# A value split ordered behind the newest weight split in the scans of a hybrid decoder step

## The chip, the cores and the metric

The kernel runs on one core of a Trainium2 chip. The metric is device microseconds from the start to the end of one execution. A profiled execution of the same program gives the traces.

## The reference

The program computes one inference step of a decoder trunk of one layer: a prompt of 256 tokens and a sample group of 8 sequences of 4 tokens, 288 tokens in all, model width 2048. The layer is a SwiGLU feed-forward block, a mixer, and a second SwiGLU block, each with a norm before and behind it. The mixer projects its input once and runs two groups of recurrences, GLA (4 heads, 128 x 256 state) and HGRN2 (8 heads, 128 x 128 state):

```python
S_t = diag(a_t) S_{t-1} + k_t^T v_t ;  o_t = q_t S_t
```

Each token reads its own update. The outputs are normalised per head, gated, concatenated and projected. Everything is float32. The outputs are both token groups and the final states of both groups; the sample group starts from given states.

## The kernel before, in words

All 288 tokens lie side by side in the free dimension. Matmuls take weights as the stationary 128 x 128 operand and tokens as the moving 128 x 288 operand. To keep float32 accuracy each operand is split into a high part and a low part, and three matmuls (lines 548, 549, 550) make one product.

**Weights.** They come in units of 128 x 1024. A unit is loaded by a DMA that SyncE issues (lines 62 and 64, tile `raw`, 3 buffers), then split: ScalarE copies `raw` to the high part `wh` (L96), and VectorE subtracts for the low part `wl` (L97). The split parts have 4 buffers, so a split waits until TensorE has done with the unit four places before. A unit feeds 24 matmuls.

**Blocks.** `block` multiplies a column block of a weight matrix: it takes the units one after the other, calls a `tick` after each 128 rows, and splits units ahead (`W.ahead`). Its four results stand in four of five PSUM banks until VectorE and ScalarE take them away. In the mixer the blocks are q and k of GLA, v of GLA, then `hfq` (forget gate and query of HGRN2) and `hi` (its values), then four gate blocks and the output projection.

**Scans.** While TensorE works on these blocks, six scans run beside it, two for GLA and four for HGRN2, each for two heads. A scan is a Python generator, and every tick advances the first one in the list by one step. It goes through eight levels: at each level VectorE multiplies decays into `Q` (L1055), `k` (L1058) and `F` (L1060), ScalarE lays copies out for the scores (L1065 and L1070 into the tile `R`), and TensorE makes scores (L995 and others). After the levels, `value_parts` splits the sample's values, then for each of two heads come `key_t` (TensorE turns the keys), `out` (outputs), `key_e` (ScalarE takes the turned keys away: `kd` L1210, `ks` L881), `apart` (VectorE masks by sequence: `bd` L1218) and `sample` (TensorE makes the state update `sn`, L1260 or L1263; VectorE adds it to the state, L1266).

**The value split.** The values of the sample tokens stand in `vs`, 32 partitions, in float32. They come there by ScalarE (L906), or, in the blocks v0, v1 and hi0, by VectorE's 32 x 32 transposes and four DMAs of GpSimd (L924); `Vh` and `Vg` are the prompt's values, moved likewise (L926). `value_parts` writes the high part twice and the low part once into one tile of 96 partitions, `Vsg` or `Vsh`: ScalarE's copy L1197, VectorE's subtraction L1198, ScalarE's copy L1199. The readers are the masked values `bd` in the HGRN scans and the matmuls `sn` in the GLA scans.

**Order.** Engines issue in order. Which order that is a list scheduler decides when the program is built: it goes by the place in the source and by a model of when each instruction could run, and can move an instruction ahead of others that come before it in the source. `tc.issue_after(ins)` adds an edge from each instruction traced in its block to `ins` where both are on the same engine; it sets the order on that engine and adds no wait between engines.

Of the kernel before, what the change touches and what calls it, by code (L numbers as in the profile page):

```python
# [9 lines left out]
F32 = mybir.dt.float32  # L10
F32R = mybir.dt.float32r
U8 = mybir.dt.uint8
AF = mybir.ActivationFunctionType
ALU = mybir.AluOpType
# [4 lines left out]
TS = 32  # L19
# [18 lines left out]
class Weights:  # L38
# [46 lines left out]
    def pieces(self, n):  # L85

        i = self.split
        raw = self.raws.pop(i)
        pool = self.extra if i in self.extra_units else self.hlp
        h = pool.tile([P, 1024], F32R, name=f"wh{i}", tag="wh")  # L90
        l = pool.tile([P, 1024], F32R, name=f"wl{i}", tag="wl")
        self.parts[i] = (h, l)
        self.split += 1
        for c in range(0, 1024, 1024 // n):
            c = slice(c, c + 1024 // n)
            i1 = self.nc.scalar.activation(h[:, c], raw[:, c], AF.Copy).ins  # L96
            i2 = self.nc.vector.tensor_tensor(l[:, c], raw[:, c], h[:, c].bitcast(F32), op=ALU.subtract).ins  # L97
            yield i1, i2

    def room(self):  # L100
# [25 lines left out]
def trunk_kernel(ctx, tc, x_prompt, x_sample, state_gla, state_hgrn, norm_gains, f1_in, f1_out, f2_in, f2_out,  # L126
# [3 lines left out]
    V, S, G, PE = nc.vector, nc.scalar, nc.gpsimd, nc.tensor  # L130
# [40 lines left out]
    W = Weights(tc, rawp, hlp)  # L171
# [604 lines left out]
    def mixer(pn, border):  # L776
        with ExitStack() as mx:
# [170 lines left out]
            def scan(d, Vt, V32, Vs, gla, ytile0, s0, sp_out, ss_out):  # L948
# [9 lines left out]
                fs, c = [d["f"]], 0  # L958
# [234 lines left out]
                def value_parts():  # L1193

                    c = slice(0, 512) if gla else slice(0, 256)
                    v = V32[0:TS, c]
                    S.activation(Vs[0:TS, c], v, AF.Copy)  # L1197
                    V.tensor_tensor(Vs[TS:2 * TS, c], v, Vs[0:TS, c].bitcast(F32), op=ALU.subtract)  # L1198
                    S.activation(Vs[2 * TS:96, c], v, AF.Copy)  # L1199

                def key_t(a):
                    tp = auxtile("tp_k")
# [116 lines left out]
                def new_state():  # L1319
                    sample(*todo.pop(0))  # L1320
                    if todo and todo[0][0] in kds:
                        apart(*todo[0])

                value_parts()
                for a in range(2):
                    tp = key_t(a)
# [135 lines left out]
            for kind, g in HORDER:  # L1462
# [8 lines left out]
                for j in list(ds):  # L1471
                    if j // 2 in vts:
                        c = slice((j % 2) * 256, (j % 2 + 1) * 256)
# [116 lines left out]
```

## Time and profile before

| | |
|---|---|
| median of 3 runs | 2254.05 us (2253.89 to 2254.5) |
| profiled execution, span from first to last instruction | 2251.7 us |
| median less span | 2.35 us |
| DMA traffic | 384.28 MB, mean 171 GB/s |
| costliest VectorE group: weight split L97 | 821.8 us in 674 |
| costliest ScalarE group: weight split L96 | 711.4 us in 674 |

The profiled execution has no run time of its own beside its span; the last difference stands for what lies around it. Lines in the fences come from the page of the profile or from views of its trace. A row of a timeline holds the start and the duration in us, the engine (PE is TensorE, PEld its weight loads, DVE is VectorE, ACT is ScalarE, POOL is GpSimd), the source line, the operation with the tile written and the tiles read, and in brackets how long the engine stood idle before it and what ended that. A row of waits holds who waited for whom, the total in us, how often, and the longest.

### The profile page before, as it was taken

How to read it: one execution, taken by the hardware profiler on the slowest of the kernel's cores; microseconds unless marked ns; L12 is line 12 of the kernel's file. 1: busy time of each engine (PE TensorE's matmuls, PEld its weight loads, DVE VectorE, ACT ScalarE, POOL GpSimd, SP SyncE). 2: the span in 40 equal slices, each digit the busy share in tenths (PEclk: the TensorE clock that was granted, in tenths of full speed). 3: DMA queues.
4: the chain of work that ended last, by engine and by line, in shares of the span. 5: the costliest groups of instructions: out<-in, count | busy, mean ns of one | idle time of the engine just before them, and what ended most of it. 6: DMA issues, size and time to landing. Idle time of an engine off the chain costs nothing.

```text
span 2251.7 us, 43317 instructions
## 1 busy us (share of the span) xinstructions
PE 2235.9 (99%) x17832; PEld 2220.0 (99%) x17832; DVE 1384.2 (61%) x2249; ACT 1023.0 (45%) x1551; POOL 170.7 (8%) x311
## 2 busy tenths in 40 slices
PE   9999999999999999999999999999999999999998
PEld 9999999999999999999999999999999999999998
DVE  7545545554565568787888755944555455545646
ACT  6443333333334345665676654543333333333344
POOL 2000000000000001333000000430000000000005
PEclk9999999999999999999999999999999999999999
DMA  7554555555555554667565554655555555555555
GB/s 222 170 163 165 169 166 163 168 166 164 167 168 180 167 169 138 192 205 201 167 176 173 171 187 132 187 185 168 167 163 167 168 163 166 168 167 164 167 166 151
DMA packets 226886, 384.28 MB, mean 171 GB/s; under 512 B 21138, under 2 KB 60736, under 8 KB 226688
## 3 DMA queue, kind: packets, MB, share of 16 engines
q1 hardware_dynamic: 214096, 365.15, 51.0%
q0 software_dynamic: 10416, 16.18, 2.7%
q8 instruction: 140, 2.29, 0.4%
q10 hardware_dynamic: 2176, 0.18, 0.1%
q14 instruction: 58, 0.48, 0.1%
HBM read 363.75 MB, written 11.80 MB: 167 GB/s over the span
## 4 chain that ended last, share of the span: by engine, by line
PE 94%; DVE 2%; ACT 1%; DMA 1%; issue 1%; POOL 0%; DVEq 0%; ACTq 0%; POOLq 0%; SPq 0%
PE gate L548 9%; PE gate L550 9%; PE gate L549 9%; PE up L550 8%; PE up L548 8%; PE out L549 8%; PE up L549 8%; PE out L550 8%; PE out L548 8%; PE mo L550 2%; PE mo L548 2%; PE mo L549 2%; PE hfq L548 1%; PE hfq L549 1%; PE hfq L550 1%; DVE wl L97 1%
## 5 line engine op out<-in xcount | busy, mean ns | idle before, releaser
L97 DVE TENSOR_TENSOR wl<-raw,wh 128x1024 fp32r<-128x1024 f32 (+1 forms) x674 | 821.8, 1220 | 619.2 <-ACT wh L96 615.2
L96 ACT ACTIVATE wh<-raw 128x1024 fp32r<-128x1024 f32 (+1 forms) x674 | 711.4, 1057 | 1021.6 <-PE gate L549 309.9
L548 PE MATMUL gate<-xh,wh 128*128 128x288 f32 x1660 | 489.2, 296 | 0.5 <-DVE z L1484 0.3
L550 PE MATMUL gate<-xh,wl 128*128 128x288 f32 x1660 | 488.7, 295 | 0.5 <-DVE wl L97 0.5
L549 PE MATMUL gate<-xl,wh 128*128 128x288 f32 x1660 | 485.3, 295 | 0.0
L549 PE MATMUL out<-hl,wh 128*128 128x288 f32 x1408 | 415.6, 295 | 0.0
L548 PE MATMUL up<-xh,wh 128*128 128x288 f32 x1408 | 414.9, 295 | 0.3 <-ACT g L618 0.2
L550 PE MATMUL up<-xh,wl 128*128 128x288 f32 x1408 | 415.1, 295 | 0.0
L550 PE MATMUL out<-hh,wl 128*128 128x288 f32 x1408 | 415.0, 295 | 0.0
L549 PE MATMUL up<-xl,wh 128*128 128x288 f32 x1408 | 414.6, 294 | 0.0
L548 PE MATMUL out<-hh,wh 128*128 128x288 f32 x1408 | 413.7, 294 | 0.0
L548 PEld LDWEIGHTS gate<-xh,wh 128*128 128x128 f32 x1660 | 311.0, 188 | 1.7 <-DVE z L1484 0.6
L550 PEld LDWEIGHTS gate<-xh,wl 128*128 128x128 f32 x1660 | 311.4, 188 | 0.9 <-DVE wl L97 0.9
L549 PEld LDWEIGHTS gate<-xl,wh 128*128 128x128 f32 x1660 | 310.4, 188 | 0.3
L548 PEld LDWEIGHTS up<-xh,wh 128*128 128x128 f32 x1408 | 264.1, 188 | 0.9 <-ACT g L618 0.7
L550 PEld LDWEIGHTS out<-hh,wl 128*128 128x128 f32 x1408 | 264.7, 188 | 0.0
L548 PEld LDWEIGHTS out<-hh,wh 128*128 128x128 f32 x1408 | 264.5, 188 | 0.0
L549 PEld LDWEIGHTS out<-hl,wh 128*128 128x128 f32 x1408 | 264.4, 188 | 0.0
L550 PEld LDWEIGHTS up<-xh,wl 128*128 128x128 f32 x1408 | 264.2, 188 | 0.0
L549 PEld LDWEIGHTS up<-xl,wh 128*128 128x128 f32 x1408 | 264.1, 188 | 0.1
L706 DVE TENSOR_TENSOR y<-out,y 128x288 f32<-128x288 f32 x288 | 121.2, 452 | 101.3 <-PE out L550 98.3
L548 PE MATMUL hfq<-xh,wh 128*128 128x288 f32 x256 | 78.1, 305 | 0.0
(391 smaller groups left out, 2516.3 us busy)
## 6 DMA issues: line engine op xcount, KB each, us to landing
raw<-in_ffn_w_in_dram SPq DMA_DIRECT2D x351, 512.0 KB, 3.5
raw<-in_ffn_w_out_dram SPq DMA_DIRECT2D x176, 512.0 KB, 3.5
raw<-in_mix_w_in_dram SPq DMA_DIRECT2D x64, 512.0 KB, 3.9
raw<-in_mix_w_in_dram SPq DMA_DIRECT2D x96, 256.0 KB, 3.1
raw<-in_mix_w_out_dram SPq DMA_DIRECT2D x32, 512.0 KB, 3.7
out_dram<-s POOLq DMA_DIRECT2D x32, 256.0 KB, 2.7
s<-in_state_gla_dram SPq DMA_DIRECT2D x16, 256.0 KB, 5.2
s<-in_state_hgrn_dram SPq DMA_DIRECT2D x16, 256.0 KB, 4.8
```

The lines of the kernel that those rows point to most:

```text
L96: i1 = self.nc.scalar.activation(h[:, c], raw[:, c], AF.Copy).ins
L97: i2 = self.nc.vector.tensor_tensor(l[:, c], raw[:, c], h[:, c].bitcast(F32), op=ALU.subtract).ins
L548: yield lambda: PE.matmul(dst, w[0][:, c:c + P], parts[0], start=start, stop=False)
L549: yield lambda: PE.matmul(dst, w[0][:, c:c + P], parts[1], start=False, stop=False)
L550: yield lambda: PE.matmul(dst, w[1][:, c:c + P], parts[0], start=False, stop=stop)
L706: V.tensor_tensor(y[k], ps, y[k], op=ALU.add)
```

## The change

The weight splitter remembers its newest pair of instructions, and the three instructions of the value split are traced under an edge to that pair:

```diff
             i1 = self.nc.scalar.activation(h[:, c], raw[:, c], AF.Copy).ins
             i2 = self.nc.vector.tensor_tensor(l[:, c], raw[:, c], h[:, c].bitcast(F32), op=ALU.subtract).ins
+            self.recent = i1, i2
             yield i1, i2
...
                     v = V32[0:TS, c]
-                    S.activation(Vs[0:TS, c], v, AF.Copy)
-                    V.tensor_tensor(Vs[TS:2 * TS, c], v, Vs[0:TS, c].bitcast(F32), op=ALU.subtract)
-                    S.activation(Vs[2 * TS:96, c], v, AF.Copy)
+                    with tc.issue_after(W.recent[0]), tc.issue_after(W.recent[1]):
+                        S.activation(Vs[0:TS, c], v, AF.Copy)
+                        V.tensor_tensor(Vs[TS:2 * TS, c], v, Vs[0:TS, c].bitcast(F32), op=ALU.subtract)
+                        S.activation(Vs[2 * TS:96, c], v, AF.Copy)
```

The two copies on ScalarE stand behind the newest `wh`, the subtraction on VectorE behind the newest `wl`. Newest is meant at the place in the source: the last unit that had been split when `value_parts` was traced. No instruction is added or removed. The scheduler, with the new edges, also places some other instructions of the scans differently.

## The prediction

> **What bounds the kernel now.** First the profile page, then the waits of TensorE over the whole span.
>
> ```profile
> span 2251.7 us, 43317 instructions
> PE 2235.9 (99%) x17832; PEld 2220.0 (99%) x17832; DVE 1384.2 (61%) x2249; ACT 1023.0 (45%) x1551; POOL 170.7 (8%) x311
> ...
> PE sc L995 <- ACT R L1070: 2.4, 1, 2.4
> PE warm L297 <- POOL onesD L228: 1.1, 1, 1.1
> PE gate L550 <- DVE wl L97: 0.5, 1, 0.5
> PE gate L548 <- DVE z L1484: 0.3, 1, 0.3
> ```
>
> TensorE is busy for 99% of the span, so an edit on another engine pays only where TensorE stands still or runs slowly. Its waits are a short list. The longest is one wait of 2.4 us, in the scans: the score matmuls of L995 wait for ScalarE's copy R of L1070. The change touches the scans, so I opened the timelines of the four engines around that place, TensorE first (start, duration, engine, line).
>
> ```profile
> 1052.36 0.29 PE L550 MATMUL hfq<-xh,wl 128*128 128x288 f32 x1
> 1055.00 0.55 PE L995 MATMUL sc<-R,k_h 128*32 128x48 f32 x32 [2.35 <-ACT R L1070]
> ...
> 1056.39 0.42 PE L548 MATMUL hfq<-xh,wh 128*128 128x288 f32 x1
> ...
> 1059.90 0.29 PE L548 MATMUL hfq<-xh,wh 128*128 128x288 f32 x1
> ...
> 1060.16 0.29 PE L550 MATMUL hfq<-xh,wl 128*128 128x288 f32 x1
> 1060.38 0.45 PE L995 MATMUL sc<-Q,k_h 128*32 128x16 f32 x32
> ...
> 1061.00 0.30 PE L549 MATMUL hfq<-xl,wh 128*128 128x288 f32 x1
> ...
> 1063.91 0.29 PE L550 MATMUL hfq<-xh,wl 128*128 128x288 f32 x1
> ```
>
> Two losses are seen here. From 1052.36 to 1055.00 nothing starts. And from 1056.39 to 1059.90 the weight matmuls start farther apart. The table by stretches (us, busy and count, granted clock, DMA share, GB/s) says why:
>
> ```profile
> 1056.39:1059.90 3.51, 3.51 (x17) 0.51 0.84 216
> 1061.00:1064.51 3.51, 3.51 (x28) 1.00 0.71 208
> ```
>
> The granted clock fell to half after the gap, and 3.51 us held 17 matmuls where they hold 28 at full clock. Why was R late? ScalarE, VectorE and GpSimd:
>
> ```profile
> 1045.23 1.06 ACT L96 ACTIVATE wh<-raw 128x1024 fp32r<-128x1024 f32 x1 [1.03 <-PE hfq L549]
> 1052.39 0.41 ACT L1197 ACTIVATE Vsh<-vs 32x256 fp32r<-32x256 f32 x1 [6.09 <-DMA vs<-y]
> 1052.71 0.40 ACT L1065 ACTIVATE R<-Q 128x256 f32<-128x256 f32 x1
> ...
> 1053.60 1.04 ACT L96 ACTIVATE wh<-raw 128x1024 fp32r<-128x1024 f32 x1
> 1054.55 0.40 ACT L1070 ACTIVATE R<-Q 128x256 f32<-128x256 f32 x1
> ...
> 1048.47 0.45 DVE L1055 TENSOR_TENSOR Q<-Q,F 128x288 f32<-128x288 f32 x1
> ...
> 1053.14 0.43 DVE L1055 TENSOR_TENSOR Q<-Q,F 128x256 f32<-128x256 f32 x1 [3.42 <-ACT R L1065]
> ...
> 1045.32 2.19 POOL L924 DMA_DIRECT2D vs<-y x4
> ```
>
> ScalarE issues in order. The scheduler had put the value split of the first HGRN scan (L1197) ahead of R (L1065). Its input vs comes by four DMAs that GpSimd issued from 1045.32 on, so ScalarE stood for 6.09 us. Behind it stood L1065, the weight split and L1070, VectorE's Q waited 3.42 us for L1065, and TensorE at last waited for L1070.
>
> **The change, part by part.** No instruction is added or removed. The three instructions of the value split, at six places (two GLA scans, four HGRN scans), get an order edge behind the newest weight split traced before them. In the built order of the changed kernel the value split no longer stands between the weight split at 1045.23 and L1065; in the HGRN scan at issue it now stands after the copy rp (L1127) and ahead of kd (L1210), several scan steps later.
>
> *What goes.* The gap: 1055.00 − 1052.36 = 2.64 us; the ordinary step from a weight matmul to a score is 1060.38 − 1060.16 = 0.22; so 2.42 us go. The slow stretch: 15 starts from 1056.39 to 1059.90, 3.51 us; at full clock 22 starts from 1061.00 to 1063.91 take 2.91, 0.132 each, so 15 take 1.98; 1.53 us go. (The counts of the table agree: 28 − 17 = 11 matmuls, 1.45 us.) Sum **3.95 us**.
>
> [...]
>
> *What is late next at the old place.* L1065 needs Q, done at 1048.47 + 0.45 = 1048.92. In the old rows ScalarE takes 0.89 us from L1065 to the weight split and 0.95 from there to L1070; from 1048.95 on that ends at 1050.79 + 0.40 = 1051.2. That weight split needs a buffer that TensorE gives back, and L1070 stands behind it; its fellow at 1045.23 shows such a wait, and a unit's 24 matmuls at 0.13 us with about 1 us of scores between put the next release, as an estimate, at 1045.2 + 3.2 + 1 = 1049.4, before its turn at 1049.84. TensorE asks at 1052.36 + 0.22 = 1052.58: 1.4 us to spare. The next score (1060.38, in the new time 1056.43) needs k_h, which the new order puts behind another weight split:
>
> ```profile
> 1057.36 1.23 DVE L97 TENSOR_TENSOR wl<-raw,wh 128x1024 fp32r<-128x1024 f32 x1 [0.40 <-ACT wh L96]
> 1058.50 0.42 DVE L1058 TENSOR_TENSOR k_h<-k_h,F 128x256 f32<-128x256 f32 x1
> ```
>
> ScalarE's half of it can start at about 1052.6 and takes 1.06; VectorE's follows at 1053.7; k_h starts 1.14 later and ends at 1055.3, 1.1 us ahead.
>
> *What the moved split costs at its new place.*
>
> ```profile
> L1197 ACT ACTIVATE Vsg<-vs x2: 630/630/631, 924.1 to 984.6; 32x512 fp32r<-32x512 f32 x2
> L1198 DVE TENSOR_TENSOR Vsh<-vs,Vsh x4: 414/416/417, 1054.3 to 1117.5; 32x256 fp32r<-32x256 f32 x4
> L1218 DVE TENSOR_TENSOR bd<-Vsh,bmask x16: 671/681/689, 1059.1 to 1248.0; 96x512 fp32r<-96x512 f32 x16
> ...
> 1070.48 0.39 ACT L1210 ACTIVATE kd<-tp_k 128x256 f32<-128x256 f32 x1 [1.03 <-PE tp_k L877]
> ...
> 1073.07 1.23 DVE L97 TENSOR_TENSOR wl<-raw,wh 128x1024 fp32r<-128x1024 f32 x1 [1.72 <-ACT wh L96]
> ...
> 1182.11 0.45 DVE L1431 SCALAR_TENSOR_TENSOR q_h<-z,lsg 128x288 f32<-128x288 f32 x1
> 1182.60 0.29 DVE L883 TENSOR_TENSOR ks<-tp_k,ks 32x128 fp32r<-32x128 f32 x1
> ...
> 1185.49 0.40 PE L1263 MATMUL sn<-bd,ks 96*128 96x512 f32 x1
> ```
>
> Behind the split on ScalarE wait kd and ks, on VectorE ks and the masked values bd; TensorE's state matmuls sn (L1263) wait for these. In the first HGRN scan ScalarE idles 1.03 us before kd, and two copies of 0.42 fit; VectorE idles 1.72 us, with 0.42 + 2 × 0.68 = 1.78 to place in it and in another gap before: nothing. The third HGRN scan is the tightest that I found: q_h to 1182.5, split to 1183.0, ks to 1183.3, first bd to 1184.0, sn at 1185.49: 1.5 us to spare. In the GLA scans the split takes 0.63 per copy, and sn needs it itself. So nothing at the six places; bounds zero and 2 × 2 × 0.63 + 4 × 2 × 0.42 = 5.9 us were every copy exposed. On SP one weight load and one state load change places; GpSimd's queue stays. I take zero for both.
>
> *A side effect.* In the last scan the scheduler now issues the first matmul for the fourth PSUM tile of a gate block after 12 matmuls of that block, not 22. It needs the fifth bank free, which VectorE's z (L1484) does.
>
> ```profile
> 1205.42 0.29 PE L548 MATMUL gate<-xh,wh 128*128 128x288 f32 x1
> ...
> 1205.87 1.22 DVE L97 TENSOR_TENSOR wl<-raw,wh 128x1024 fp32r<-128x1024 f32 x1
> 1207.01 0.82 DVE L946 SCALAR_TENSOR_TENSOR lsg<-z,ls 128x288 f32<-128x288 f32 x2
> 1207.75 0.45 DVE L1484 TENSOR_TENSOR z<-gate,rt 128x288 f32<-128x288 f32 x1
> ```
>
> TensorE arrives at 1205.42 + 12 × 0.132 = 1207.0. z ended at 1208.20; the new order moves the weight split (1.14) behind it, which puts z's end near 1207.0 and, with two small products moved either way, perhaps at 1206.8. That is level: cost nothing, at most 1208.2 − 1207.0 = 1.2 us.
>
> The sum is made against the profiled execution, whose span is 2251.7; the runs' median 2254.05 lies 2.35 above it, taken as the same before and after. 2254.05 − 3.95 = **2250.1 us**, 0.18% faster.
>
> **The rivals.**
> *Longer stall in plain runs.* The stall ends when the vs DMAs land, in a crowded stretch, so its length is a matter of queueing. The table of DMA issues (last column: median us to landing) shows
>
> ```profile
> Vh<-y POOLq DMA_DIRECT2D x9, 32.0 KB, 5.2
> ...
> Vh<-y POOLq DMA_DIRECT2D x16, 32.0 KB, 4.5
> ```
>
> from 1045 to 1053 and from 1036 to 1070: the values' DMAs take 5.2 us to land in the crowd and 4.5 in the wider stretch. Were vs in plain runs that difference of 0.7 us later, the gain would be 4.65: 2249.4. Against it: one profile says nothing of others; the three runs lie within 0.6 us.
> *No slow clock in plain runs.* The gap of 2.64 us may or may not halve the clock; the list's other gaps did not bring a second such stretch in the scans. Then only 2.42 goes: 2251.6. [...]
> *Level turns late.* The PSUM tile waits its 1.2 us: 2251.3. A later R that keeps half of the gap, so that the change does only part of what it says, gives about the same, 2252.
> *Slower.* The value split now queues behind a weight split that itself waits for TensorE's buffer. If its readers are due first, TensorE waits at all six places: 5.9 us, and if each wait halves the clock as the old one did, 6 × 1.53 more; 15.1 − 3.95 = 11.1: 2265. It decides where sn comes sooner after the split than 1.5 us; the rows above show 1.5 and more.
>
> **How the numbers follow.** A difference of 0.2%, 4.5 us, is about what a measurement of this kernel can tell from no change. Forecast 0.52; longer stall 0.23; no slow clock 0.09; late tile or partial 0.08; slower 0.08. The range from 2249.1 to 2252.0 holds all but the slower case and the ends of the others. Faster by over 0.2% needs 2249.5 or less: the longer stall and a little of the forecast, 0.27. Slower 0.08. Within 0.2%: 0.65.
>
> **What would show it.** In the profile after: no wait of L995 for R L1070 in TensorE's list, granted clock 1.00 around 1056, L1065 soon after Q, L1197 next to kd with no wait for vs. A wait of sn for bd or of a gate matmul for z over 1 us, or a second stretch at half clock, would prove the zeros wrong.

## The result and the profile after

The changed kernel takes **2250.81 us** (median of 17 runs, 2250.16 to 2251.48); the kernel before took 2254.68 beside it (17 runs, 2253.89 to 2256.72). The ratio is **0.9982, 95% interval 0.9975 to 0.9988**: 3.87 us less. The forecast was 2250.1, in a range from 2249.1 to 2252.0.

The page of the profile after opens with

```profile
span 2249.0 us, 43324 instructions
...
PE 2234.9 (99%) x17832; PEld 2218.2 (99%) x17832; DVE 1384.5 (62%) x2249; ACT 1023.0 (45%) x1551; POOL 170.1 (8%) x311
```

and TensorE's waits (waiter, releaser, total us, times, longest) with

```profile
PE warm L298 <- POOL onesD L229: 1.1, 1, 1.1
PE gate L551 <- DVE wl L97: 0.6, 2, 0.5
PE up L549 <- ACT g L619: 0.6, 2, 0.4
PE gate L549 <- DVE z L1486: 0.3, 1, 0.3
```

The wait of 2.4 us for R is gone, and no wait for `bd`, `ks` or the values took its place. (Lines of the changed kernel are one higher from L98 on and two higher behind the value split: L995 is now L996, L1070 is L1071, L1197 is L1199.) TensorE's timeline at the old place:

```profile
1053.24 0.29 PE L551 MATMUL hfq<-xh,wl 128*128 128x288 f32 x1
1053.45 0.55 PE L996 MATMUL sc<-R,k_h 128*32 128x48 f32 x32
...
1057.09 0.29 PE L551 MATMUL hfq<-xh,wl 128*128 128x288 f32 x1
1057.31 0.45 PE L996 MATMUL sc<-Q,k_h 128*32 128x16 f32 x32
```

The step into the score is now 0.21 us. From the weight matmul ahead of this score to the next score it takes 1057.31 − 1053.24 = 4.07 us; before it was 1060.38 − 1052.36 = 8.02, with the same 24 weight matmuls between the two scores in both built orders. **3.95 us** went here, which is the sum of the prediction to the digit shown. The same two stretches of time as before show the clock (us, busy and count of PE, PEld, DVE, ACT, POOL, granted clock, DMA share, GB/s):

```profile
1056.39:1059.90 3.51, 3.51 (x56) 3.32 (x55) 2.40 (x7) 1.48 (x2) 2.30 (x4) 1.00 1.09 293
1061.00:1064.51 3.51, 3.51 (x56) 3.25 (x55) 2.22 (x4) 2.38 (x8) 0.00 (x0) 1.00 0.63 170
```

ScalarE's timeline shows L1066 right behind its Q, the weight split and R behind it without a gap, and the value split only at 1066.26, with no wait for `vs`:

```profile
1049.90 0.42 ACT L1066 ACTIVATE R<-Q 128x256 f32<-128x256 f32 x1 [2.72 <-DVE Q L1056]
...
1050.81 1.04 ACT L96 ACTIVATE wh<-raw 128x1024 fp32r<-128x1024 f32 x1
1051.76 0.40 ACT L1071 ACTIVATE R<-Q 128x256 f32<-128x256 f32 x1
1053.43 1.06 ACT L96 ACTIVATE wh<-raw 128x1024 fp32r<-128x1024 f32 x1 [1.27 <-PE hfq L550]
...
1066.26 0.40 ACT L1199 ACTIVATE Vsh<-vs 32x256 fp32r<-32x256 f32 x1
...
1067.40 0.38 ACT L1212 ACTIVATE kd<-tp_k 128x256 f32<-128x256 f32 x1 [0.30 <-PE tp_k L878]
```

The spans differ by 2.7 us and not by 3.95. Laid side by side, TensorE's instructions stand 0.85 us later in the profile after at 38 us, in the first weight blocks, far from the change, 3.1 us earlier behind the stall, and 2.9 us earlier at TensorE's end. The profiled execution of the kernel before was a short one: the times of the runs lie 1.7 to 1.9 us above their spans, which puts it, as an estimate, at 2251.7 + 1.8 = 2253.5, against the median of 2254.68; the profile after is of a run at the median. The runs' medians differ by 3.87.

### The profile page after: what moved, and what is told of

It reads as the page before. It is cut to its first block, busy times and chain, and to the rows that moved or that the text cites. A ratio compares the mean times of both kernels' runs of the same rounds, so it can differ in the third digit from the quotient of the medians.

```text
span 2249.0 us, 43324 instructions
## 1 busy us (share of the span) xinstructions
PE 2234.9 (99%) x17832; PEld 2218.2 (99%) x17832; DVE 1384.5 (62%) x2249; ACT 1023.0 (45%) x1551; POOL 170.1 (8%) x311
## 4 chain that ended last, share of the span: by engine, by line
PE 94%; DVE 2%; ACT 1%; issue 1%; DMA 1%; POOL 0%; DVEq 0%; ACTq 0%; SPq 0%; POOLq 0%
PE gate L549 9%; PE gate L551 9%; PE gate L550 9%; PE up L551 8%; PE up L549 8%; PE out L550 8%; PE up L550 8%; PE out L551 8%; PE out L549 8%; PE hfq L549 2%; PE hfq L551 2%; PE hfq L550 2%; PE mo L551 2%; PE mo L549 2%; PE mo L550 2%
## 5 line engine op out<-in xcount | busy, mean ns | idle before, releaser
L672 POOL DMA_DIRECT2D zT<-b x40 | 23.2, 586 | 722.2 <-issue 721.7
```

What stands on the lines that cost most here:

```text
L672: queues[n % len(queues)].dma_start(dst[q * TS:(q + 1) * TS, 4 * g:4 * g + 4, :, cols].rearrange("p k t c -> p (k t) c"), b32[rows, q])
```

## The experiments

Theory: the whole gain is one wait of ScalarE's in-order queue for the DMAs of `vs`, 6.09 us long, at one place, and the slow clock behind it, 0.51 of full in the stretch of 3.51 us; only an order that keeps every such split from that place gains. Rivals: each of the six places gives a part; the gain comes from other instructions that the edges move; VectorE's half counts. A second question was what a late R costs in general, and when the clock falls to half.

The prediction had left one thing out. It says that the stalling instruction is the split of the first HGRN scan, and that is so: in the built order of the kernel before, the copy ahead of L1065 reads columns 0 to 255 of `vs`, those of the first scan. But two HGRN scans read the values of the block hi0, and the split of the second (columns 256 to 511) stood close behind, after R of L1070:

```profile
1055.39 0.42 ACT L1197 ACTIVATE Vsh<-vs 32x256 fp32r<-32x256 f32 x1
```

What it does when the first alone is held, the prediction did not ask. In the first six experiments the edge is put on some of the scans or on one engine, against the changed kernel.

**The first two HGRN scans alone (e6).**

```diff
-                    with tc.issue_after(W.recent[0]), tc.issue_after(W.recent[1]):
+                    two = not gla and ytile0 < 12
+                    with tc.issue_after(W.recent[0]) if two else ExitStack(), tc.issue_after(W.recent[1]) if two else ExitStack():
```

> The edge is put only on the value splits of the first two HGRN scans (the two that read the values of block hi0); the other four scans are as in the kernel before. Theory (ScalarE stood in order at these splits until their DMAs landed, TensorE then stood 2.4 us for R and ran at half clock): the whole gain is here, so no wait of the score matmul for R, granted clock 1.00 around 1056, and about 2250.8 us, ratio 0.998 to the kernel before. Rival A (all six places give a part each): about a third of the gain, 2253.4. Rival B (the gain is the other placing of instructions late in the scans): 2254.7.

Measured: 2250.71 us beside 2254.22, ratio 0.9984 (0.9975 to 0.9993). No wait of the score, and full clock in the stretch that was slow:

```profile
1056.40:1059.81 3.41, 3.41 (x55) 3.22 (x55) 2.30 (x7) 1.48 (x2) 2.29 (x4) 1.00 1.10 287
```

Two of six edges carry the gain.

**The first HGRN scan alone (e1), all but the first (e2), and the other four (e7).** The condition `two` becomes, in e1, e2 and e7 in turn,

```diff
+                    first_h = not gla and ytile0 == 8
+                    rest = not (not gla and ytile0 == 8)
+                    rest = not (not gla and ytile0 < 12)
```

> The edge is put only on the value split of the first HGRN scan, the one that the prediction named. In its built order the split of the second HGRN scan now stands between the weight split and the copy of L1065, and reads values that come by the same DMAs. Theory: it waits there just as long, so the score still waits 2.0 to 2.6 us for R, the clock falls to half, and the time stays at about 2254.7, ratio 1.000. Rival (the stall belongs to the first scan's split, as the prediction says): 2250.8, ratio 0.998.

> The edge is put on all value splits but that of the first HGRN scan. In its built order the first scan's split stands ahead of the copy of L1065. Theory: the stall and the half clock stay, about 2254.7, ratio 1.000, though five of six splits are held. Rival A (each place gives a sixth of the gain): 2251.5. Rival B (only the second scan's split counts): 2250.8.

> The edge is put on the other four value splits: two GLA scans and the last two HGRN scans. Theory: nothing is gained, the score waits 2.4 us for R as before, clock at half behind it, 2254.7, ratio 1.000; a delay of up to 0.2 us at the fourth PSUM tile of a gate block may show. Rival A (each place gives a part): two thirds of the gain, 2252.1. Rival B (the gain is the later placing): 2250.8.

Measured, beside 2254.22 us of the kernel before: e1 2254.83 us, ratio 1.0002 (0.9993 to 1.0011); e2 2254.89, 1.0004 (0.9995 to 1.0012); e7 2254.55, 1.0003 (0.9994 to 1.0012). None gains. ScalarE's and TensorE's timelines of e1:

```profile
1053.42 0.41 ACT L1200 ACTIVATE Vsh<-vs 32x256 fp32r<-32x256 f32 x1 [6.52 <-DMA vs<-y]
1053.75 0.40 ACT L1066 ACTIVATE R<-Q 128x256 f32<-128x256 f32 x1
...
1056.04 0.55 PE L996 MATMUL sc<-R,k_h 128*32 128x48 f32 x32 [2.78 <-ACT R L1071]
```

The first scan's split is held, so this L1200 is the second scan's, which the scheduler has now put ahead of L1066, and it stands for the same DMAs. In e2 it is the first scan's:

```profile
1055.97 0.41 ACT L1200 ACTIVATE Vsh<-vs 32x256 fp32r<-32x256 f32 x1 [6.98 <-DMA vs<-y]
...
1058.58 0.55 PE L996 MATMUL sc<-R,k_h 128*32 128x48 f32 x32 [3.24 <-ACT R L1071]
```

Each of the two is enough for the stall, so it takes both edges to remove it. The shares of a sixth, a third or two thirds are refuted, and so is the rival that holding the first scan's split alone would do. (In e7 another score also waited 0.8 us for `k_h`; its cause is not shown.)

**One engine's edge alone (e3, e4).**

```diff
-                    with tc.issue_after(W.recent[0]), tc.issue_after(W.recent[1]):
+                    with tc.issue_after(W.recent[0]):
```

and for e4 the same with `W.recent[1]`.

> Only ScalarE's edge is kept (behind the newest wh); VectorE's edge (behind the newest wl) is left out. Theory (the wait of ScalarE's in-order queue is what counts): the full gain, no wait for R, 2250.8 us, ratio 0.998. Rival (VectorE's subtraction at its early place holds the copy Q or k_h back for the same DMAs): a wait of the score stays, 2252 to 2254.7.

> Only VectorE's edge is kept; ScalarE's is left out, so that the split's copies stay ahead of L1065 on ScalarE. Theory: the stall stays, 2254.7, ratio 1.000, the score waits 2.0 to 2.6 us for R. Rival (VectorE's queue is what counts): 2250.8.

Measured: e3 2250.03 us beside 2253.61, ratio 0.9984 (0.9975 to 0.9992); e4 2253.32 beside the same, ratio 1.000 (0.9991 to 1.0009). In e4 the row of TensorE is

```profile
1055.60 0.55 PE L996 MATMUL sc<-R,k_h 128*32 128x48 f32 x32 [2.96 <-ACT R L1071]
```

ScalarE's queue is the whole of it; VectorE's edge does nothing that can be measured.

**Other data, no edge (e5).** Against the kernel before:

```diff
-                    v = V32[0:TS, c]
+                    v = x[0][0:TS, c] if not gla and ytile0 < 12 else V32[0:TS, c]
```

> The kernel before, without any edge, but the value splits of the first two HGRN scans read a part of the input x in place of the values vs (so the sample updates of these heads use other values): they wait for no DMA of GpSimd. The scheduler then places them early, behind the values' splits of GLA, and no longer ahead of L1065. Theory: no wait for R, clock 1.00, about 2250.8, ratio 0.998. Rival (the gain of the change is in other placings that the edges bring): 2254.7.

Measured: 2249.58 us beside 2253.61, ratio 0.9983 (0.9974 to 0.9992). The view of line 1197 (count: shortest, median and longest ns, first and last start) shows the two splits 66 us earlier:

```profile
L1197 ACT ACTIVATE Vsh<-x x2: 417/417/417, 986.0 to 986.8; 32x256 fp32r<-32x256 f32 x2
```

Without an edge the same gain comes. The split is harmless early, when its data is there, and late, when its data has come; it hurts only ahead of other work while the DMAs are on their way. This kernel changes the position along with the data, so it does not tell the two apart; that the place alone matters is shown by e1 to e4.

**Making R late by known work (d3 to d9).** In the changed kernel the copy L1071 (in these kernels L1072) is repeated in the first HGRN scan, three to nine times more:

```diff
-                    S.activation(near, src, AF.Copy)
+                    for _ in range(4 if not gla and ytile0 == 8 else 1):
+                        S.activation(near, src, AF.Copy)
```

with 5, 7, 8 and 10 in place of 4 for d4, d6, d7 and d9. The 3.413, 1.98 and 1.59 us in the expectations are read from the five profiles with the stall, which stand below.

> The changed kernel with the copy of L1070 made four times in place of once in the first HGRN scan: three more copies of about 0.4 us on ScalarE, all ahead of R's end. The estimated spare time of R there is 1.25 to 1.4 us. Theory: R comes 1.2 us later, just within the spare time: a wait of the score of 0 to 0.4 us, no half clock, 2250.8 to 2251.2. Rival (spare time much smaller): a wait of 1 us or more, 2252; rival (a late copy always costs as much as in the kernel before): 2254.7.

> The changed kernel with four more copies of L1070 in the first HGRN scan: three ahead of the next weight split, as in d3_three_copies, and one behind it, so that R comes late by ScalarE's own work and not by a DMA. R should end about 1055.0 where TensorE stands from 1053.9 on: a wait of about 1.1 us. Theory (the clock is judged in fixed windows of 3.413 us; a window with 1.98 us of standstill or more is followed by one at half clock, one with 1.59 or less is not; where the windows lie differs from run to run): never a half clock, so 1.15 us above d3_three_copies, about 2.8 us below the kernel before (ratio 0.9988), and runs close together. Rival (any late copy costs as much as in the kernel before): ratio 1.000.

> As d4_four_copies, with three copies behind the weight split: a wait of about 1.9 us. Theory (fixed windows, limit between 1.59 and 1.98 of 3.413 us): half clock in about half of the runs at most, none where the wait is cut by a window's edge; 2.0 us above d3_three_copies in the runs without and 3.5 in those with, about 1.1 us below the kernel before in the middle (ratio 0.9995). [...]

> As d4_four_copies, with four copies behind the weight split: a wait of about 2.35 us, as in the kernel before. Theory (fixed windows): half clock in about two runs of three, as in the kernel before, and about the time of the kernel before less 0.5 us, whose stall varies with its DMAs (ratio 0.9998); in the profile the idle time within the fixed windows, counted from the first instant of full clock, tells whether one follows at half clock. [...]

> As d4_four_copies, with six copies behind the weight split: a wait of about 3.2 us. Theory (fixed windows): half clock in about nine runs of ten, 3.25 + 1.5 = 4.75 us above d3_three_copies, about 0.8 us above the kernel before (ratio 1.0004). [...]

Measured: d3 2249.73 us beside 2253.61, ratio 0.9982 (0.9973 to 0.9991); the others beside 2253.77: d4 2249.79, 0.9982 (0.9973 to 0.9991); d6 2249.74, 0.9982 (0.9973 to 0.9991); d7 2250.35, 0.9984 (0.9975 to 0.9993); d9 2249.80, 0.9983 (0.9974 to 0.9991). d3 came as expected, with no wait and the full gain. For d4 to d9 **neither the theory nor the rival of d4 held**: there is no wait of the score, and no slow clock behind it (from the second on, the weight matmuls there start 0.12 to 0.14 us apart; at full clock before it was 0.132). In d9 R is late enough, on ScalarE and then on TensorE:

```profile
1049.56 0.42 ACT L1066 ACTIVATE R<-Q 128x256 f32<-128x256 f32 x1 [2.73 <-DVE Q L1056]
...
1054.06 2.65 ACT L1072 ACTIVATE R<-Q 128x256 f32<-128x256 f32 x6
...
1056.47 0.29 PE L551 MATMUL hfq<-xh,wl 128*128 128x288 f32 x1
1056.76 0.55 PE L996 MATMUL sc<-R,k_h 128*32 128x48 f32 x32
```

R ends at 1054.06 + 2.65 = 1056.71, and the score starts at 1056.76, with a weight matmul 0.29 us ahead of it. The built orders say why. In the kernels before and after the score stands behind the 264th weight matmul of the block; in d3 behind the 266th, in d4 the 275th, in d6 the 282nd, in d7 the 285th and in d9 the 291st. The scheduler, which sees the copies when it builds the order, put the score 27 matmuls later in d9, and TensorE did weight matmuls meanwhile. My expectation had kept the score at its old place. So in these five kernels an R that was late by planned work cost nothing that can be measured. The stall of the kernel before looks like one that the scheduler had not foreseen (its model of the DMAs is not shown): the score stood behind the 264th matmul, as if `vs` were there in time, while the DMAs, issued until 1045.32 + 2.19 = 1047.51, let the split start only at 1052.39, 4.88 us later. These runs therefore say nothing of the slow clock, and the gap could not be set to a chosen length.

**When the clock falls to half** can be read from the five profiles that have the stall. In the profile before the half clock lasted from 1056.395 to 1059.808, 3.413 us. Its changes fell on a grid of that step, counted from the first instant of full clock near the start of the kernel, 5.09 us: (1056.395 − 5.09) / 308 = 3.41333, and 5.09 + 308 × 3.41333 = 1056.40, where the half clock began. In e2 it is 5.29 + 309 × 3.41333 = 1060.01. (The first instants of full clock in e4, e1 and e7 are 5.06, 6.55 and 7.10.) Laid on each profile's own grid, these are the windows with the gap and the one behind them. The kernel before, e4 and e2:

```profile
1049.57:1052.98 3.41, 3.08 (x24) 2.84 (x22) 0.15 (x1) 0.59 (x2) 2.40 (x5) 1.00 1.09 285
1052.98:1056.40 3.42, 1.40 (x39) 1.34 (x40) 3.20 (x10) 3.35 (x11) 3.00 (x6) 1.00 0.54 114
1056.40:1059.81 3.41, 3.41 (x17) 3.41 (x16) 3.01 (x11) 0.92 (x1) 1.23 (x3) 0.50 0.84 213
```

```profile
1052.95:1056.36 3.41, 0.76 (x34) 0.70 (x35) 2.61 (x9) 3.33 (x10) 3.17 (x6) 1.00 0.59 126
1056.36:1059.78 3.42, 3.42 (x16) 3.42 (x16) 2.81 (x10) 1.52 (x3) 1.45 (x3) 0.50 0.73 182
```

```profile
1053.19:1056.60 3.41, 2.15 (x17) 1.92 (x15) 0.00 (x0) 0.63 (x3) 1.49 (x3) 1.00 1.01 265
1056.60:1060.01 3.41, 1.43 (x39) 1.37 (x40) 3.23 (x10) 3.36 (x9) 3.41 (x7) 1.00 0.34 60
1060.01:1063.43 3.42, 3.42 (x16) 3.42 (x15) 3.42 (x13) 0.04 (x1) 0.73 (x2) 0.50 0.84 220
```

and e1 and e7, where the same kind of gap brought no half clock:

```profile
1051.04:1054.45 3.41, 2.21 (x17) 1.98 (x15) 0.27 (x1) 1.02 (x5) 1.96 (x4) 1.00 1.03 266
1054.45:1057.86 3.41, 1.82 (x42) 1.76 (x43) 3.35 (x12) 3.01 (x6) 3.41 (x7) 1.00 0.43 76
1057.86:1061.28 3.42, 3.42 (x55) 3.23 (x55) 3.30 (x13) 1.41 (x2) 0.34 (x1) 1.00 0.92 248
```

```profile
1051.58:1054.99 3.41, 2.12 (x17) 1.89 (x15) 0.86 (x4) 1.61 (x7) 2.16 (x4) 1.00 1.00 265
1054.99:1058.41 3.42, 2.42 (x46) 2.36 (x47) 2.95 (x11) 3.25 (x6) 3.25 (x7) 1.00 0.44 78
1058.41:1061.82 3.41, 3.36 (x55) 3.09 (x54) 3.41 (x11) 1.06 (x1) 0.22 (x1) 1.00 1.01 271
```

The first number behind the comma, PE's busy time, is what to read, with the granted clock of the row below. Windows in which TensorE was busy for 1.40, 0.76 and 1.43 us, that is idle for 2.0, 2.65 and 1.98, are followed by one at half clock; windows with 2.21, 1.82, 2.15, 2.12 and 2.42 busy, idle for at most 1.59, are not. The gap's length does not order the cases: 2.35 us in the kernel before was followed by half clock, 2.78 in e1 was not; there a window's edge cut it into 1.20 and 1.59. That agrees with all five stalls; it was found in them, and d4 to d9 gave it no test.

As a limit on busy time it does not hold at the end of the kernel. There, where the weight matmuls run out, the clock falls to half too, and on the grid: at 2244.23 us in the profile before and at 2240.34 in the profile after, 656 and 655 windows behind the first full clock (5.09 and 4.61). In the windows before these two falls TensorE was busy for 0.52 and 1.40 us. In e3 the window before that fall was busy for 2.94 us, idle for only 0.47, and the clock fell all the same:

```profile
2234.61:2238.02 3.41, 2.94 (x25) 2.49 (x23) 2.03 (x5) 2.32 (x6) 0.58 (x2) 1.00 0.00 0
2238.02:2241.43 3.41, 0.00 (x0) 0.00 (x0) 3.41 (x7) 0.36 (x2) 0.00 (x0) 0.50 0.81 297
```

Of its 25 matmuls 22 are small, 128 x 1 or 128 x 128, where the weight matmuls are 128 x 288. So the busy time that the profile shows is not by itself what the clock goes by, the bounds of 1.59 and 1.98 us hold for these five stalls alone, and what it does go by stays open.

## Why the prediction was right

- *What binds.* One wait of L995 for R, caused by ScalarE standing 6.09 us for `vs`: right, shown by e3 against e4. That the split of the first scan was the one is right too, by the built order. What it left out is the second scan's split, which takes the place when the first alone is held (e1). The price was not touched by that, as the change holds both.
- *The gap, 2.42, and the slow stretch, 1.53.* Together 3.95 predicted and 3.95 measured between the same two scores. Both go by the same profile before, so this shows that the whole of its loss there went, not that every execution loses as much. The other stalls, of 2.78, 3.24, 2.28 and 2.96 us, show that it varies. With 0.07 added to each for the step from start to start, and 1.53 for the three of five in which the clock was halved, the five have a mean of 2.79 + 0.92 = 3.7 us. The medians of the eight kernels without the stall lie 3.4 to 4.0 us under those of the kernel before beside them.
- *The spare time of R at the old place, 1.4.* R ended at 1051.76 + 0.40 = 1052.16; TensorE asked at 1053.24 + 0.22 = 1053.46: 1.3. The weight split between followed without a wait, as estimated. For the next score 1.1 was predicted:

```profile
1055.67 0.42 DVE L1059 TENSOR_TENSOR k_h<-k_h,F 128x256 f32<-128x256 f32 x1
```

  it ended at 1056.09, 1.2 us ahead of 1057.31.
- *The moved split costs nothing.* Right: no `sn` wait, and e6, which puts no edge on four of the six splits, has the same ratio within its interval as the full change (0.9984 and 0.9982).
- *Median less span, 2.35, taken as the same.* It was 1.8 in the profile after, and 1.7 to 1.9 in the other runs. This did not touch the forecast, which takes 3.95 from the median.
- *The fourth PSUM tile, 0 to 1.2.* Its wait for z is 0.3 us before and after: nothing. Side by side the two traces drift apart by 0.18 us there, and this is back 20 us later.
- *Chances.* "Longer stall in plain runs" and "no slow clock in plain runs" were put as rivals to one forecast. The five profiles show them to be two sides of one scatter: some executions have the half clock and some don't, and the stall lies between 2.28 and 3.24 us. The runs agree: those of the kernel before spread over 2.8 us, those of the changed one over 1.3. That the sum from one profile came so near to the difference of the medians is partly luck: worked out in the same way, e7's profile would have given 2.35 and e2's 3.31 + 1.53 = 4.84. The forecast lies 0.7 us under the measured 2250.81, of which 0.6 is that the kernel before ran at 2254.68 in this measurement and not at 2254.05.

## What to carry to other kernels

Where engines issue in order, the instruction that waits for a DMA must not stand ahead of work that TensorE needs soon: here ScalarE stood 6.09 us for `vs`, and TensorE 2.35 us for the R behind it. Look for it at the engine two steps back from TensorE's wait, and check that no fellow of it takes the free place when it is moved. Here the scheduler filled TensorE with other matmuls and so made the delays that it could plan for free; what remained to be found was one that its order did not allow for, the landing of four small DMAs. Price such a stall with the half clock that may follow (it did in three of the five stalls, 1.53 us by the profile before), and take several profiles: the same stall cost between 2.4 us and 4.8 in five of them.

## What the runs showed of the hardware that was not expected

The granted clock changed only on a grid of 3.413 us, after 308, 309 and 656 windows in the profile before and after 655 in the profile after, counted from its first full clock. A standstill of 2.35 us was followed by half clock for one window, and one of 2.78 us, cut by an edge of the grid into 1.20 and 1.59, was not. At the end of e3 a window that was busy for 2.94 of 3.41 us, mostly with small matmuls, was followed by half clock too. The four DMAs of `vs`, of 16 KB each, let their reader start 4.9 us after the end of their issue in the profile before, and 5.8 us (1055.97 less 1048.01 + 2.19) in that of e2.
